# Where the 64-place and the 32-place expert stand in the order of a routed feed-forward stage

## The chip, the cores and the metric

One core of one Trainium2 chip runs the whole kernel as a single program. The metric is the device time of one execution in microseconds (us), from the device's own record; the median of several runs is compared. TensorE (PE in the rows, its weight loads PEld) does the matmuls, VectorE (DVE), ScalarE (ACT) and GpSimd (POOL) the rest, and SyncE's queue (SP) issues the loads of the weights.

## The reference

Two layers of a decoder on 256 tokens of width 1024, all in 32-bit floats. Each layer has a token mixer (four kinds of attention), a normalisation, a channel mixer, a normalisation and a small gated product with a per-layer embedding. The channel mixer of layer 0 is one dense SwiGLU. That of layer 1 is routed: every token goes to the best two of eight experts, and an expert is a SwiGLU of inner width 3584. Cut to what matters:

```python
def swiglu(x, w1, w3, w2):
    return (jax.nn.silu(x @ w1) * (x @ w3)) @ w2
...
        if i % 2 == 0:
            f = swiglu(h, ffn_w1[i // 2], ffn_w3[i // 2], ffn_w2[i // 2])
        else:
            f = moe_swiglu(h, moe_router[i // 2], moe_w1[i // 2], moe_w3[i // 2], moe_w2[i // 2])
        h = layer_norm(DEEPNORM_ALPHA * h + f, ln_ffn_g[i], ln_ffn_b[i])
        h = h + jax.nn.sigmoid(h @ ple_gate[i]) * (p[i] @ ple_proj[i])
```

All eight experts' weights (8 x 3 x 1024 x 3584 x 4 bytes, 352 MB) are read once from device memory.

## The kernel before, in words

The routed stage ranks the experts by how many tokens they got. The expert of rank r has `PLACES[r]` places for tokens: (128, 128, 96, 96, 96, 64, 32, 32). Ranks 0 and 1 are of class `Big`: their weights are split into a high and a low part (ACT line 103, DVE line 111) and each product is three matmuls (lines 142 to 144). The others are of class `Small`: plain 32-bit matmuls read the weights as they landed (line 1269 for `w1` and `w3`, line 1323 for `w2`). With fewer places than 128, one chunk of weights is worked on by several column groups of the array side by side (`q`: 4 groups of 32 places, or 2 of 64), so a chunk costs the less time the fewer places the expert has.

An expert is worked on in column steps of its inner width. A `Big` or 96-place expert has four steps (1024, 1024, 1024, 512 columns), a 64- or 32-place expert two (2048, 1536). `STEPS` lists pairs (rank, step) in the order of the work. One turn of the loop over `STEPS` does, in this order: `up` with `w1` of its own step (in its middle, `turn_last` transposes the previous step's result, lines 1194 and 1294); SiLU on ACT; `down` with `w2` of the *previous* step; `up` with `w3` of its own step and the scaling by the gates; then `make_for(s)`, which prepares an expert that comes later (`gather`: the tokens' rows are picked by matmuls with a 0/1 matrix, lines 1134 and 1135, transposed, line 1140, and the gates are gathered, line 1108); then `finish_last`, which puts an expert's result back to its tokens (`put_back`, lines 1117 and 1340, added to the residual by `add_back` on DVE, line 1353), if the previous step was that expert's last. The recording layer interleaves such pieces into the matmuls around them.

The tokens `x` of an expert lie in a tile `xg` (two halves for two experts each) or, for 32 places, in a tile `xe`. The `xg` tiles of the 96- and 64-place experts use the memory of the `Big` experts' tiles, so none of them can be made before the last matmul of (1,3) with `w3` has read those. After the last step `closing()` loads what the end of layer 1 needs, `put_back` of the last expert follows, a branch (line 1441) leads round a fallback for a fuller routing, and the second normalisation and the embedding product end the kernel.

The weights come in 348 chunks of 1 MB, or 768 KB for the second step's `w1` and `w3` of 64- and 32-place experts, all issued by SP's queue in the order of use (line 87; two pieces of 512 KB each from line 1314 where a group's rows don't lie together). `load_raw` takes twelve buffers (`raw` 4, `side` 3, `post` 3, `early` 2) in a fixed rotation: a chunk's load waits until the chunk twelve places ahead of it has been used. A chunk of either size takes a whole buffer.

Of the kernel before, what the change touches and what calls it, by code (L numbers as in the profile page):

```python
# [22 lines left out]
D_FF, N_EXP = 3584, 8  # L23
NFC = D_FF // 512
PLACES = (128, 128, 96, 96, 96, 64, 32, 32)
STEPS = ((0, 0), (7, 0), (0, 1), (0, 2), (0, 3), (1, 0), (7, 1), (1, 1), (1, 2), (1, 3), (6, 0), (2, 0),
         (2, 1), (2, 2), (2, 3), (6, 1), (3, 0), (3, 1), (3, 2), (5, 0), (3, 3), (4, 0), (4, 1), (4, 2),
         (4, 3), (5, 1))
PLE = 256
ALPHA = (2 * DEPTH) ** 0.25  # L30
EPS = 1e-5
# [22 lines left out]
def body(ctx, tc, nc, I, out):  # L54
# [932 lines left out]
    def swiglu_moe(hT, logits, closing):  # L987
        hh, hl = hT
        with tc.tile_pool(name="moe", bufs=1, reuse_waits="tile") as mp:
# [131 lines left out]
            def gather(r, n, off, x):  # L1121


                oh = places(r, n, off)
                if off == 0 and r == 0:
                    with tc.issue_after(done["oh"].ins):
                        gates()
                        ranks()
                xs = mp.tile([128, D], FT, name="xs", tag="xs", bufs=1)
                for f in range(2):  # L1130
                    fs = slice(f * 512, (f + 1) * 512)
                    p = work()
                    for t in range(NT):
                        nc.tensor.matmul(p[:n], oh[:, t], hsh[:, t, fs], start=t == 0, stop=False)
                        nc.tensor.matmul(p[:n], oh[:, t], hsl[:, t, fs], start=False, stop=t == NT - 1)
                    nc.scalar.activation(xs[:n, fs], p[:n], AF.Copy)
                for k0 in range(0, KD, 4):
                    p = work()[:, :4 * n].rearrange("p (a b) -> p a b", a=4)
                    for j in range(4):
                        nc.tensor.transpose(p[:, j], xs[:n, (k0 + j) * 128:(k0 + j + 1) * 128], ident[:n, :n])  # L1140
                    if n == 128:
                        ins = split_sb(x[0][:, k0:k0 + 4], x[1][:, k0:k0 + 4], p)
                    else:
                        nc.scalar.activation(x[:, k0:k0 + 4], p, AF.Copy)
                if off == 0 and r == 0:
                    table("silu_and_others", ins)
                gs = mp.tile([128, 3], FT, name="gs", tag="gs", bufs=3)
                if n == 128:
                    gates_of(r, oh, gs[:, :1])
                    return gs, back_of(oh)  # L1150
                w = 64 if n == 64 else 32
                for j in range(n // w):
                    gates_of(r, places(r, w, off + j * w, 128 // w), gs[:, j:j + 1])
                return gs, None
# [205 lines left out]
            def experts_in(base, order):  # L1360
                sizes = [128] * N_EXP if base else PLACES
                seq = STEPS if base == 0 else [(r, c) for r in range(N_EXP) for c in range(len(Big.cols))]
                first = {}
                for s, (r, c) in enumerate(seq):
                    first.setdefault(r, s)
                made = {}

                xg = {}

                def half(kind, i, j):  # L1370
                    if kind not in xg:
                        xg[kind] = [pers.tile([128, KD, 256], kind, name="xg", tag=tag) for tag in ("hTh", "hTl")]
                    return xg[kind][i][:, :, j * 128:(j + 1) * 128]

                def make(r):
                    n = sizes[r]
                    if n == 128:
                        x = [half(FR, i, r % 2) for i in range(2)]
                    elif n > 32:
                        x = half(FT, r in (3, 4), r in (4, 5))  # L1380
                    else:
                        x = mp.tile([128, KD, 32], FT, name="xe", tag="xe", bufs=1)
                    if n < 128:
                        x = x[:, :, :n]
                    got = gather(r, n, PLACES[r] if base else 0, x)
                    made[r] = Big(r, x, got) if n == 128 else Small(r, x, got, n)

                def make_for(s):
                    for r, f in first.items():
                        if f and max(f - 2, 0) == s and r not in made:  # L1390
                            make(r)

                make(seq[0][0])
                if base == 0:
                    order.enter_context(tc.issue_after(done["oh"].ins))
                    order.enter_context(tc.issue_after(done["hs"].ins))
                if base == 0:
                    for t in range(NT):
                        nc.vector.tensor_scalar(h[:, t], h[:, t], ALPHA, None, op0=OP.mult)
                before_ = g = gT = None  # L1400

                def turn_last():
                    nonlocal gT
                    if g is not None:
                        gT = before_[0].turn(g, before_[1])

                def finish_last():
                    ex, c = before_
                    if c == len(ex.cols) - 1:
                        ex.put_back()  # L1410

                for s, (r, c) in enumerate(seq):
                    now = made[r]
                    ps = now.up("moe_w1", c, turn_last)
                    sl = mp.tile([128, 1024], FT, name="sl", tag="sl")
                    for f, p in enumerate(ps):
                        nc.scalar.activation(sl[:, f * 512:f * 512 + p.shape[1]], p, AF.Silu)
                    if before_ is not None:
                        before_[0].down(gT, before_[1])
                    elif s == 0:  # L1420
                        make_for(s)
                    now.scale(sl, now.up("moe_w3", c))
                    if before_ is not None:
                        make_for(s)
                        finish_last()
                    g, before_ = sl, (now, c)
                    if s == 0 and base == 0:
                        turn_last()
                        now.down(gT, c)
                        g = before_ = None  # L1430
                turn_last()
                before_[0].down(gT, before_[1])
                rest = closing() if base == 0 else None
                finish_last()
                if rest is not None:
                    rest()
# [12 lines left out]
    for i in range(DEPTH):  # L1449
        hT, got = mixer(i, hT, None if i else second)  # L1450
        with tc.tile_pool(name=f"post{i}", bufs=1, reuse_waits="tile") as pool:
# [7 lines left out]
            else:  # L1459
# [7 lines left out]
                def closing():  # L1467

                    for n in ("early", "post", "side"):
                        del rings[n]  # L1470
                    n = PLE // 128 * S
                    words = held()
                    kept["p"] = [words[:, j * n:(j + 1) * n].rearrange("p (k s) -> p k s", s=S).bitcast(FR)
                                 for j in range(2)]
                    ple_turn(i, pool.tile([128, NT, PLE], FT, name="pt", tag="sg", bufs=1), *kept["p"])
                    kept["proj"] = ple_weights(i, held)
                    raw = load_raw(gate_weights(i, 0)[:, :4], [128, 4, 512])
                    kept["gb"] = load_gb("ffn", i, halves(held()))
                    kept["gate"] = []

                    def split(u):
                        wh, wl = split_unit(raw[:, u:u + 2], held, nc.gpsimd)
                        kept["gate"] += [(wh[:, j], wl[:, j]) for j in range(2)]

                    split(0)
                    return lambda: split(2)
# [47 lines left out]
```

## Time and profile before

| what | value |
|---|---|
| median of 3 runs | 1522.1 us (1520.16 to 1522.77) |
| the profiled execution's own time | 1520.21 us |
| its span in the profile | 1518.4 us |
| PE busy | 1429.0 us, 94% of the span |
| DVE, ACT busy | 681.5 us (45%), 563.0 us (37%) |
| loads by SP's queue | 455.5 MB, packets busy 77.5% of 16 engines' span |
| mean granted clock of TensorE | 0.97 |

The profiled execution took 1.8 us more than its span, and 1.9 us less than the median of the runs. Shares are averages over a span with several stages; the routed stage runs from about 600 to 1472 us.

### The profile page before, as it was taken

The numbers are of one execution on the slowest core, as the hardware profiler recorded it, in microseconds if no ns is written. First come the engines' busy times: TensorE is split into PE (matmuls) and PEld (weight loads), VectorE is DVE, ScalarE is ACT, GpSimd is POOL, SyncE is SP. The second block draws the span as 40 slices with busy tenths as digits, with TensorE's granted clock in tenths as the row PEclk, the third lists the DMA queues.
The fourth block names the chain that finished last, engine by engine and source line by source line (L and its number), as shares of the span: only waits on it lengthen the run. The fifth ranks groups of instructions, "written<-read, shape, count | busy, mean of one in ns | idle before, by whom it ended". The sixth has DMA issues, their size and how long they took to land. (4 is left out here: it accounts for less than half of the span.)

```text
span 1518.4 us, 29609 instructions
## 1 busy us (share of the span) xinstructions
PE 1429.0 (94%) x12545; PEld 993.4 (65%) x12545; DVE 681.5 (45%) x1167; ACT 563.0 (37%) x877; POOL 9.3 (1%) x16
## 2 busy tenths in 40 slices
PE   7999899999999997979999799899899999999988
PEld 6677788888786775647876575365745544566536
DVE  7666654554776768527885584100111000010035
ACT  5465544444554566426754573000000000000024
POOL 0000000000000000000000000000000000000000
PEclk9999999999999998998999899999989999999999
DMA  8543655464256543999999998999999999999963
GB/s 288 212 153 132 222 195 193 166 204 156 99 169 219 189 153 115 374 416 412 407 377 406 411 410 354 415 411 409 388 411 410 412 419 411 408 412 398 365 237 112
DMA packets 125963, 457.46 MB, mean 301 GB/s; under 512 B 11072, under 2 KB 22144, under 8 KB 104832
## 3 DMA queue, kind: packets, MB, share of 16 engines
q1 hardware_dynamic: 125824, 455.50, 77.5%
q8 instruction: 101, 1.65, 0.5%
q14 instruction: 38, 0.31, 0.1%
HBM read 454.42 MB, written 1.05 MB: 300 GB/s over the span
## 5 line engine op out<-in xcount | busy, mean ns | idle before, releaser
L111 DVE TENSOR_TENSOR wlo<-raw,whi 128x1024 fp32r<-128x1024 f32 (+1 forms) x152 | 181.0, 1211 | 82.2 <-ACT whi L103 77.4
L103 ACT ACTIVATE whi<-raw 128x1024 fp32r<-128x1024 f32 (+1 forms) x152 | 155.9, 1051 | 109.3 <-PE acc L143 53.0
L1278 DVE SCALAR_TENSOR_TENSOR sl<-sl,gs,wk 128x256 f32<-128x256 f32 (+3 forms) x44 | 19.3, 486 | 353.5 <-PE wk L1269 353.4
L1295 ACT ACTIVATE ge<-wk 128x512 f32<-128x512 f32 (+2 forms) x29 | 13.5, 503 | 321.3 <-PE wk L1294 321.3
L1269 PE MATMUL wk<-raw,xg 128*32 128x256 f32 (+3 forms) x1800 | 104.9, 362 | 4.3 <-issue 3.6
L142 PE MATMUL wk<-whi,xg 128*128 128x512 f32 x224 | 92.2, 412 | 9.8 <-ACT whi L103 7.5
L111 DVE TENSOR_TENSOR wlo<-post,whi 128x1024 fp32r<-128x1024 f32 x70 | 84.2, 1220 | 32.8 <-ACT whi L103 31.1
L142 PE MATMUL acc<-whi,gh 128*128 128x512 f32 x224 | 88.5, 396 | 5.0 <-ACT whi L103 4.0
L103 ACT ACTIVATE whi<-post 128x1024 fp32r<-128x1024 f32 x70 | 72.6, 1057 | 54.1 <-PE wk L143 32.0
L142 PE MATMUL wk<-whi,hTh 128*128 128x512 f32 x224 | 88.6, 396 | 3.1 <-ACT whi L103 3.1
L143 PE MATMUL wk<-whi,xg 128*128 128x512 f32 x224 | 91.2, 407 | 0.0
L111 DVE TENSOR_TENSOR wlo<-side,whi 128x1024 fp32r<-128x1024 f32 x72 | 86.4, 1219 | 10.5 <-ACT whi L103 5.5
L144 PE MATMUL wk<-wlo,hTh 128*128 128x512 f32 x224 | 88.0, 394 | 0.1
L143 PE MATMUL acc<-whi,gl 128*128 128x512 f32 x224 | 87.9, 393 | 0.0
L143 PE MATMUL wk<-whi,hTl 128*128 128x512 f32 x224 | 87.6, 391 | 0.0
L1269 PEld LDWEIGHTS wk<-raw,xg 128*32 128x32 f32 (+1 forms) x1800 | 58.3, 112 | 42.1 <-issue 14.7
L144 PE MATMUL wk<-wlo,xg 128*128 128x512 f32 x224 | 84.2, 410 | 0.9 <-DVE wlo L111 0.8
L144 PE MATMUL acc<-wlo,gh 128*128 128x512 f32 x224 | 84.5, 394 | 0.3
L103 ACT ACTIVATE whi<-side 128x1024 fp32r<-128x1024 f32 x72 | 74.5, 1056 | 19.9 <-PE acc L143 12.0
L142 PE MATMUL acc<-whi,hTh 128*128 128x512 f32 (+1 forms) x192 | 77.1, 402 | 1.4 <-ACT whi L103 1.4
L144 PE MATMUL acc<-wlo,hTh 128*128 128x512 f32 (+1 forms) x192 | 76.5, 399 | 1.4 <-DVE wlo L111 1.4
L1269 PE MATMUL wk<-side,xg 128*32 128x256 f32 (+2 forms) x1216 | 73.6, 365 | 4.0 <-issue 4.0
(404 smaller groups left out, 2504.8 us busy)
## 6 DMA issues: line engine op xcount, KB each, us to landing
raw<-in_moe_w_dram SPq DMA_DIRECT2D x96, 1024.0 KB, 17.9
side<-in_moe_w_dram SPq DMA_DIRECT2D x73, 1024.0 KB, 17.8
post<-in_moe_w_dram SPq DMA_DIRECT2D x72, 1024.0 KB, 16.9
early<-in_moe_w_dram SPq DMA_DIRECT2D x49, 1024.0 KB, 17.6
raw<-in_ffn_w_dram SPq DMA_DIRECT2D x19, 1024.0 KB, 5.1
raw<-in_w_in_dram SPq DMA_DIRECT2D x15, 1024.0 KB, 7.8
post<-in_ffn_w_dram SPq DMA_DIRECT2D x14, 1024.0 KB, 5.0
raw<-in_moe_w_dram SPq DMA_DIRECT2D x17, 768.0 KB, 10.9
```

The costliest lines, as they stand in the source:

```text
L103: nc.scalar.activation(hi, v, AF.Copy)
L111: engine.tensor_sub(lo, v, hi.bitcast(FT))
L142: nc.tensor.matmul(ps, xh, wh, start=first, stop=False)
L143: nc.tensor.matmul(ps, xl, wh, start=False, stop=False)
L144: return nc.tensor.matmul(ps, xh, wl, start=False, stop=last)
L1269: nc.tensor.matmul(ps[b][self.rows(u), at:at + wd], self.x[:, k, self.block(j)], raw[:, k % m, u * w + o:u * w + o + wd], start=k == 0 and ...
L1278: nc.vector.scalar_tensor_tensor(sl[:, fs], sl[:, fs], self.gs[:, j:j + 1], ps[b][:, at:at + wd], op0=OP.mult, op1=OP.mult)
L1295: nc.scalar.activation(gT[:, j0:j0 + m], p, AF.Copy)
```

## The change

Ranks 5 (64 places) and 6 (32 places) swap their places in `STEPS`, so that the 64-place steps stand behind (1,3) and behind (2,3), and the 32-place steps stand ahead of (4,0) and at the end. (3,3) no longer has another expert's step ahead of it. In `make_for` the expert of rank 5 is made one step ahead of its first step, not two, because its tile needs the memory that (1,3) still reads. No size, no buffer and no arithmetic on any expert changes.

```diff
-STEPS = ((0, 0), (7, 0), (0, 1), (0, 2), (0, 3), (1, 0), (7, 1), (1, 1), (1, 2), (1, 3), (6, 0), (2, 0),
-         (2, 1), (2, 2), (2, 3), (6, 1), (3, 0), (3, 1), (3, 2), (5, 0), (3, 3), (4, 0), (4, 1), (4, 2),
-         (4, 3), (5, 1))
+STEPS = ((0, 0), (7, 0), (0, 1), (0, 2), (0, 3), (1, 0), (7, 1), (1, 1), (1, 2), (1, 3), (5, 0), (2, 0),
+         (2, 1), (2, 2), (2, 3), (5, 1), (3, 0), (3, 1), (3, 2), (3, 3), (6, 0), (4, 0), (4, 1), (4, 2),
+         (4, 3), (6, 1))
...
-                        if f and max(f - 2, 0) == s and r not in made:
+                        if f and (f - 1 if r == 5 and not base else max(f - 2, 0)) == s and r not in made:
```

First place: PE at the seam between (1,3) and the step behind it. `xg_4858` and `xg_4859` are the `Big` tiles, `oh` the 0/1 matrix, `xs` the gathered rows. Before, the seam holds the end of making expert 2 and then the 32-place step's first matmuls:

```order
L144 MATMUL wk_7478<-wlo_7514,xg_4858 128x512
L1135 MATMUL wk_7530<-hsl_4816,oh_7526 96x512
L1134 MATMUL wk_7536<-hsh_4815,oh_7526 96x512
L1135 MATMUL wk_7536<-hsl_4816,oh_7526 96x512
L1134 MATMUL wk_7536<-hsh_4815,oh_7526 96x512
L1135 MATMUL wk_7536<-hsl_4816,oh_7526 96x512
L1140 MATMUL wk_7542<-ident_69,xs_7529 128x96 x4
L1140 MATMUL wk_7548<-ident_69,xs_7529 128x96 x4
L1108 MATMUL wk_7558<-gate_r_4855,oh_7555 128x1 x2
L1108 MATMUL wk_7565<-gate_r_4855,oh_7562 128x1 x2
L1108 MATMUL wk_7572<-gate_r_4855,oh_7569 128x1
L1269 MATMUL wk_7576<-raw_7577,xe_7290 32x512
```

At the same place of the changed kernel, the end of making expert 5 comes first and then the making of expert 2; behind these rows come one more of line 1140, the gates of line 1108 and then the 64-place step's first matmuls (line 1269, `raw,xg`, 64x512):

```order
L1140 MATMUL wk_7505<-ident_69,xs_7492 128x64 x4
L1140 MATMUL wk_7511<-ident_69,xs_7492 128x64 x4
L1108 MATMUL wk_7521<-gate_r_4855,oh_7518 128x1 x2
L1134 MATMUL wk_7529<-hsh_4815,oh_7525 96x512
L1135 MATMUL wk_7529<-hsl_4816,oh_7525 96x512
L1134 MATMUL wk_7529<-hsh_4815,oh_7525 96x512
L1135 MATMUL wk_7529<-hsl_4816,oh_7525 96x512
L1134 MATMUL wk_7535<-hsh_4815,oh_7525 96x512
L1135 MATMUL wk_7535<-hsl_4816,oh_7525 96x512
L1134 MATMUL wk_7535<-hsh_4815,oh_7525 96x512
L1135 MATMUL wk_7535<-hsl_4816,oh_7525 96x512
L1140 MATMUL wk_7541<-ident_69,xs_7528 128x96 x4
```

Expert 5 is now made here, one step ahead of its use, where expert 6 had been made one step earlier, and expert 2 is made whole between the two.

Second place: PE at the end of the routed stage, `down` of the last step and `put_back` of its expert. Before, with 64 places:

```order
L1294 MATMUL wk_12542<-ident_69,sl_12335 128x128 x2
L1323 MATMUL acc_10767<-post_12546,ge_12535 64x512 x4
L1323 MATMUL acc_10767<-raw_12552,ge_12535 64x512 x4
L1323 MATMUL acc_10767<-raw_12558,ge_12535 64x512 x4
L1323 MATMUL acc_10767<-side_12564,ge_12535 64x512 x4
L1323 MATMUL acc_10767<-post_12570,ge_12535 64x512 x4
L1323 MATMUL acc_10767<-early_12576,ge_12535 64x512 x4
```

The changed kernel has 32 places there:

```order
L1294 MATMUL wk_12502<-ident_69,sl_12304 128x128 x3
L1323 MATMUL acc_11069<-post_12507,ge_12501 32x256 x8
L1323 MATMUL acc_11069<-raw_12517,ge_12501 32x256 x8
L1323 MATMUL acc_11069<-raw_12527,ge_12501 32x256 x8
L1323 MATMUL acc_11069<-side_12538,ge_12501 32x256 x8
L1323 MATMUL acc_11069<-post_12548,ge_12501 32x256 x8
L1323 MATMUL acc_11069<-early_12558,ge_12501 32x256 x8
```

The six last chunks are the same in number and buffers, and each now has eight matmuls of 256 columns in four column groups instead of four of 512 columns in two. `put_back` behind them has 16 matmuls of 256 columns and eight `add_back` of 128x256 where it had eight of 512 columns and four of 128x512.

## Rows read from the trace of the kernel before

**Rows 1.** The page, 40 slices of the span: mean DMA rate

```profile
GB/s 288 212 153 132 222 195 193 166 204 156 99 169 219 189 153 115 374 416 412 407 377 406 411 410 354 415 411 409 388 411 410 412 419 411 408 412 398 365 237 112
```

**Rows 2.** Windows of 20 us: busy us by engine, granted clock, DMA share, GB/s

```profile
920.00:940.00 20.00, 18.67 (x109) 10.45 (x111) 4.31 (x14) 2.65 (x5) 0.00 (x0) 0.91 0.76 301
...
980.00:1000.00 20.00, 17.15 (x260) 9.22 (x256) 1.03 (x3) 0.00 (x0) 0.00 (x0) 0.83 1.02 408
1000.00:1020.00 20.00, 20.00 (x358) 11.93 (x354) 0.23 (x1) 1.74 (x4) 0.00 (x0) 1.00 1.02 415
...
1400.00:1420.00 20.00, 18.93 (x461) 13.78 (x455) 0.00 (x0) 1.36 (x3) 0.00 (x0) 1.00 1.00 386
1420.00:1440.00 20.00, 17.50 (x179) 8.36 (x174) 0.86 (x3) 1.36 (x3) 0.00 (x0) 0.91 0.92 346
```

**Rows 3.** PE's timeline, neighbouring chunks of one size: start us, us

```profile
957.25 1.04 PE L1269 MATMUL wk<-raw,xe 128*32 128x512 f32 x8
958.11 1.04 PE L1269 MATMUL wk<-side,xe 128*32 128x512 f32 x8
...
1428.10 1.46 PE L1269 MATMUL wk<-post,xg 128*64 128x512 f32 x8
1429.39 1.46 PE L1269 MATMUL wk<-early,xg 128*64 128x512 f32 x8
...
1468.94 1.89 PE L1323 MATMUL acc<-post,ge 128*64 128x512 f32 x8
1470.66 1.89 PE L1323 MATMUL acc<-early,ge 128*64 128x512 f32 x8
```

**Rows 4.** SP's timeline, DMA issues (us to landing), PE's timeline: first chunk of (6,0)

```profile
886.61 0.34 SPq L87 DMA_DIRECT2D raw<-in_moe_w_dram  x1
...
raw<-in_moe_w_dram SPq DMA_DIRECT2D x1, 1024.0 KB, 18.3
...
920.81 13.58 SPq L87 DMA_DIRECT2D raw<-in_moe_w_dram  x2
...
930.88 1.04 PE L1269 MATMUL wk<-raw,xe 128*32 128x512 f32 x2
```

**Rows 5.** PE's timeline with its waits: `w2` of (6,0), first and last wait

```profile
974.49 1.07 PE L1323 MATMUL acc<-side,ge 128*32 128x256 f32 x16 [1.23 <-DMA side<-in_moe_w_dram]
...
987.14 4.34 PE L1269 MATMUL wk<-post,xg 128*32 128x256 f32 x48 [1.59 <-DMA post<-in_moe_w_dram]
```

**Rows 6.** The same three views: first chunks of (6,1) and of (5,1)

```profile
1060.19 8.96 SPq L87 DMA_DIRECT2D post<-in_moe_w_dram  x1
...
post<-in_moe_w_dram SPq DMA_DIRECT2D x1, 768.0 KB, 19.3
...
1097.21 0.83 PE L1269 MATMUL wk<-post,xe 128*32 128x384 f32 x2
...
1390.01 5.75 SPq L87 DMA_DIRECT2D raw<-in_moe_w_dram  x1
...
raw<-in_moe_w_dram SPq DMA_DIRECT2D x1, 768.0 KB, 16.1
...
1423.78 2.82 PE L1269 MATMUL wk<-raw,xg 128*64 128x512 f32 x8 [2.50 <-issue]
```

**Rows 7.** The same views at the end: last weights, then PE and DVE

```profile
1446.15 0.33 SPq L87 DMA_DIRECT2D early<-in_moe_w_dram  x1
...
early<-in_moe_w_dram SPq DMA_DIRECT2D x1, 1024.0 KB, 11.8
...
1472.48 0.66 PE L280 MATMUL wk<-ident,pt 128*128 128x128 f32 x4
...
1474.93 0.49 PE L1340 MATMUL wk<-yl,ohT 64*128 64x512 f32 x2
...
1481.14 0.68 DVE L1353 SCALAR_TENSOR_TENSOR h<-h,wk 128x512 f32<-128x512 f32 x1
...
1482.03 0.77 PE L142 MATMUL acc<-early 128*128 128x512 f32 x1 [6.62 <-DVEq L1441]
```

## The prediction

> **What bounds the kernel now.** I began with the slices of the page [rows 1]. From about slice 17 on, roughly 600 us into the span, the weights arrive at some 410 GB/s almost without a break until the last slices: the routed stage is bound by its stream of weights. Then I read windows of 20 us, to see where the stream falls short of that [rows 2]. An undisturbed window moves 415 GB/s at a DMA share of 1.02; the stretch 920 to 940 only 301, and 1400 to 1440 only 386 and 346. Such dips have one kind of cause here, and the reader sees it at the first of them [rows 4]: SP's queue stands for 13.58 us from 920.81 on, because the buffer that its load wants is still in use by PE. PE was far behind. The first chunk of (6,0) was issued at 886.61 and landed 18.3 us later, at 904.9, but its first matmul starts at 930.88. I call that distance PE's *lag* behind the stream: 26.0 us. With twelve buffers a lag of that size leaves nothing to load into.
>
> So the stage has two ledgers. The stream ends when all chunks have been moved at 410 GB/s, plus every us in which no buffer was free. And PE ends some lag after the stream. Last I read the end [rows 7]: the last weights were issued at 1446.15 and landed 11.8 us later, at 1458.0, while PE finished with them at 1472.5. The end of the stage is therefore set by PE, 14.5 us behind the stream.
>
> **The price of a chunk.** At 410 GB/s a chunk of 1 MB takes the stream 2.56 us and one of 768 KB 1.92 us. On PE, by the distance of neighbouring starts [rows 3], 1 MB takes 0.86 us with 32 places and 1.72 with 64, and 768 KB takes 1.29 us with 64. So every such chunk lets PE catch up, a 32-place chunk by 1.70 us, a 64-place one by 0.84. The arithmetic of all experts is the same before and after; the change only moves where PE catches up, and 24 chunks of a first step are worth 40.8 us of it with 32 places, 20.2 with 64.
>
> **At the end: the gain.** The last step (6,1) takes 0.86 us a chunk against 2.56 of the stream, so PE will be waiting for each of the last chunks and be done one chunk's work after the last landing: 0.9 us behind instead of 14.5. If the stream ended when it does now, that would be 13.6 us gained. Bounds of that lag: 0.9, and 4 if the transposes of the step's result come late.
>
> **Behind (1,3): the lag that stays.** Before, PE went through the 24 chunks of (6,0) (and `w1` of (2,0) and `w2` of (1,3) among them) and its lag fell from 26.0 to nothing: from 974.49 to 987.14 it waited six times for a chunk, 6.1 us in all [rows 5]. So part of that catching up was wasted. The ledger closes as follows: 26.0, plus what PE did besides in this stretch, less 40.8 caught up, less the stream's own loss (20 us at 301 instead of 410 GB/s is 5.3) must give -6.1; the rest is 14.0 us. With (5,0) there instead: 26.0 + 14.0 - 20.2 - 5.3 = 14.5 us of lag at `w3` of (2,0), where it is now nothing. Making expert 5 in front of the step instead of expert 6 a step earlier adds no new kind of work: its matmuls take the place of similar ones that already stood ahead of 930.88. But buffers come free at 1.72 instead of 0.86 us a chunk while the queue stands. For that I take s1 = 2 us of further loss (bounds 0, since 1.72 is still quicker than the stream, and 3). The lag left is then about 12.5.
>
> **Ahead of (5,1): the first price.** In the trace of before, PE's lag grew from nothing at 987 to 17.7 at the start of (6,1) [rows 6]: that chunk was issued at 1060.19, landed at 1079.5, and was used at 1097.21. Expert 2 and the making of expert 3 stand there unchanged. 12.5 + 17.7 = 30.2 us is more than the buffers allow. At 26.0 the queue stands [rows 4], so at least 4.2 us are lost. And (5,1) brings chunks of 768 KB, which fill a whole buffer with less stream: where they were the next to load, a lag of 17.7 was already enough to take the stream to 346 GB/s (the first chunk of (5,1) was issued at 1390.01, landed 16.1 later, used at 1423.78 [rows 6, 2]). Down to that level it would be 12.5 us lost. I take s2 = 9, since a window of mixed sizes lies between the two levels and nearer to the small chunks: 26.0 x 0.75 is 19.5, from which 30.2 stands off by 10.7.
>
> **Ahead of (6,0): the second price.** Expert 3 now runs its four steps in one piece, without the 64-place step that stood between (3,2) and (3,3), and expert 4 is made directly in front of (6,0), as expert 2 was in front of (6,0) before. No row gives the lag that it comes with. The nearest is that very dip, 5.3 us; I take s3 = 5 (bounds 0, if the lag is still under 20, and 7, with two more us for the making).
>
> **What goes away.** The losses of 1400 to 1440 belong to (5,1) with a PE that was 17.7 behind: 20 x (410 - 386)/410 + 20 x (410 - 346)/410 = 1.2 + 3.1 = 4.3 us. Behind (6,0) PE is close to the stream, so most of it should go: 3 us (bounds 0 and 4.3).
>
> **The sum.** The stream ends at 1458.0 + 2 + 9 + 5 - 3 = 1471.0, and PE at 1471.9 instead of 1472.5: -0.6 us. In the tail, `put_back` of the 32-place expert has eight `add_back` of 256 columns where four of 512 took 0.68 each [rows 7]; at most the double, 2.7 us more, at least nothing. The closing loads now come right behind weights that PE waits for, and no longer 14 us ahead of the branch at 1482.03. I take 1.3 us for both together. That makes +0.7 us: 1520.9 against the profiled 1520.2. The profiled execution lies 1.9 us under the median of the runs, so against the median the forecast is 1522.8 us: no change that can be told. What a measurement of this kernel can tell from no change is about 0.2%, 3 us.
>
> **A clock rule that speaks against the change.** Where PE waited for single chunks, its clock fell: the window 980 to 1000 has a granted clock of 0.83, so for a third of it PE ran at 1.2 instead of 2.4 GHz [rows 2, 5]. The Trainium skill, "TensorE: Matmul & The Clock Gate", section "HAM oscillation — how this bites in real kernels", describes this pattern: a loop whose matmuls are done before the next tile of weights has come drops to the low clock in the wait and starts each next tile slow. The trace agrees. Here the last 32-place step is such a loop. At the low clock a chunk takes 1.72 us, still under 2.56, so only the last chunk (+0.9) and the matmuls of `put_back` would show, which stand between 1472.48 and 1475.4 with a pause among them [rows 7]: 2 us more at the most. That is some +3 us on the sum, 1525.8.
>
> **Rivals.** *The buffers absorb it (0.25).* If the lag ahead of (5,1) is only carried and worked off, what is left of s1, s2, s3 is the necessary 4.2, and the loss at the end goes: 1458.0 + 4.2 - 3 = 1459.2, PE at 1460.1, 12.4 earlier, less 1.3 in the tail: 1511.0; with s1 as well 1513.0, in the middle 1512.0. For it: while the lag grew from nothing to 17.7, the stream moved its 415 GB/s [rows 2]. Against: at 26.0 it stood. *The middle costs more than the end gives (0.20).* One mechanism, at one place: the 768 KB chunks of (5,1). If the queue stands until the lag is down to 17.7, s2 is 12.5 and the stream then meets (6,0) with the full s3 of 7: 2 + 12.5 + 7 - 3 = 18.5, PE ends at 1477.4, +4.9 and 1.3, 1528.3; with s1 at 3 and nothing gone away at the end, 1532. It decides where the losses together pass 12.3 us (13.6 less the tail's 1.3). *The low clock at the end (0.10)*: 1525.8, as above. *The exchange as summed: 0.45*, 1519.8 to 1525.8.
>
> **How the numbers follow.** Faster by over 0.2%: the first rival and a little of the exchange, 0.28. Slower: the second rival, most of the third, 0.29. Within: 0.43. The range goes from the first rival's 1512 to the second's 1530; beyond them I leave a part of each, together under 0.2. The exchange's own range is 1519.8 to 1525.8.
>
> **What would show it.** In the profile of the changed kernel: the last weights land at about 1471 and PE is done with them within 2 us, with a wait for DMA ahead of each of the last chunks; no wait for DMA in `w2` of (5,0), where there were six; dips of the GB/s ahead of (5,1), some 1080 to 1120, and ahead of (6,0), some 1240 to 1280; none at 1400 to 1440. The forecast is wrong if the dip ahead of (5,1) is under 4 us or over 13, or if the end still shows PE more than 4 us behind.

## The result: slower by 0.6%

| | before | changed |
|---|---|---|
| median | 1520.75 us (1516.69 to 1522.77, 6 runs) | 1528.55 us (1525.41 to 1532.05, 6 runs) |
| ratio, 95% interval | | 1.0057 (1.0036 to 1.0078) |
| profiled execution | 1520.21 us, span 1518.4 | 1528.78 us, span 1527.0 |

The kernel became 7.8 us slower by the medians, 8.6 us by the two profiled spans. The forecast was 1522.8 us with a range of 1512 to 1530: the time lies in the range, near its upper end, but outside the exchange's own 1519.8 to 1525.8. It stands at the second rival (the middle costs more than the end gives, 1528.3 us).

The windows of 20 us of the changed kernel, with the columns of [rows 2], show where the stream of weights stood:

```profile
920.00:940.00 20.00, 18.25 (x76) 10.11 (x76) 3.75 (x17) 3.41 (x7) 0.00 (x0) 0.74 0.51 195
940.00:960.00 20.00, 18.29 (x74) 9.01 (x70) 6.09 (x7) 6.66 (x9) 0.00 (x0) 0.91 1.00 404
...
1080.00:1100.00 20.00, 18.97 (x464) 14.03 (x466) 0.00 (x0) 1.36 (x3) 0.00 (x0) 1.00 0.95 360
1100.00:1120.00 20.00, 18.67 (x118) 10.01 (x109) 2.99 (x14) 2.54 (x5) 0.00 (x0) 0.83 0.58 195
...
1240.00:1260.00 20.00, 19.68 (x398) 14.10 (x394) 2.26 (x8) 2.97 (x7) 0.00 (x0) 1.00 0.97 370
1260.00:1280.00 20.00, 18.20 (x358) 14.89 (x350) 2.44 (x11) 2.06 (x4) 0.00 (x0) 1.00 0.89 342
1280.00:1300.00 20.00, 18.68 (x190) 7.33 (x189) 2.92 (x11) 3.11 (x7) 0.00 (x0) 0.92 0.84 329
...
1400.00:1420.00 20.00, 20.00 (x458) 14.24 (x454) 1.26 (x3) 1.36 (x3) 0.00 (x0) 1.00 1.03 403
1420.00:1440.00 20.00, 17.79 (x390) 12.01 (x383) 0.86 (x3) 0.49 (x1) 0.00 (x0) 1.00 1.02 410
...
1460.00:1480.00 20.00, 12.93 (x136) 4.69 (x135) 2.60 (x9) 1.70 (x5) 0.00 (x0) 0.83 1.02 406
```

The last column is the one to read. Measured against 410 GB/s, the first pair loses 10.5 + 0.3 us where the kernel before lost 5.3 [rows 2]; the second pair 2.4 + 10.5 us, where the same windows of before moved 382 and 398 GB/s, 2.0 us; the third group 2.0 + 3.3 + 4.0 us, where the kernel before, at 418, 412 and 405 GB/s, lost nothing. And 1400 to 1440, 4.3 us short before, is now 0.3 short. Together 5.5 + 10.9 + 9.3 - 4.0 = 21.7 us more are lost than before.

The rows of the changed kernel that answer to [rows 4] and [rows 7], from SP's timeline, the DMA issues (us to landing) and PE's timeline:

```profile
883.07 0.35 SPq L87 DMA_DIRECT2D raw<-in_moe_w_dram  x1
...
raw<-in_moe_w_dram SPq DMA_DIRECT2D x1, 1024.0 KB, 18.6
...
919.66 17.04 SPq L87 DMA_DIRECT2D raw<-in_moe_w_dram  x2
...
931.27 1.97 PE L1269 MATMUL wk<-raw,xg 128*64 128x512 f32 x2
...
1069.68 2.02 SPq L87 DMA_DIRECT2D post<-in_moe_w_dram  x1
...
post<-in_moe_w_dram SPq DMA_DIRECT2D x1, 768.0 KB, 12.4
...
1106.62 1.97 PE L1269 MATMUL wk<-post,xg 128*64 128x512 f32 x2
...
1238.03 0.34 SPq L87 DMA_DIRECT2D post<-in_moe_w_dram  x1
...
post<-in_moe_w_dram SPq DMA_DIRECT2D x1, 1024.0 KB, 10.7
...
1278.71 0.62 PE L1269 MATMUL wk<-post,xe 128*32 128x512 f32 x1
...
1461.55 0.33 SPq L1314 DMA_DIRECT2D early<-in_moe_w_dram  x1
...
early<-in_moe_w_dram SPq DMA_DIRECT2D x1, 512.0 KB, 15.6
...
1472.16 1.94 PE L1323 MATMUL acc<-side,ge 128*32 128x256 f32 x16 [2.41 <-DMA side<-in_moe_w_dram]
1474.65 1.93 PE L1323 MATMUL acc<-post,ge 128*32 128x256 f32 x16 [0.56 <-DMA post<-in_moe_w_dram]
...
1478.10 0.66 PE L280 MATMUL wk<-ident,pt 128*128 128x128 f32 x4
...
1489.59 0.77 PE L142 MATMUL acc<-early 128*128 128x512 f32 x1 [8.99 <-DVEq L1441]
```

The first chunk of (5,0) landed at 901.7 and was used at 931.27, a lag of 29.6 us where it had been 26.0, and the queue stood for most of 17.04 us (that row, like the one of 13.58 us in [rows 4], holds two issues and the stand between them). The first chunk of (5,1) landed at 1082.1 and was used at 1106.62, a lag of 24.5; that of (6,0) landed at 1248.7 and was used at 1278.71, a lag of 30.0. At the end the last piece of the weights landed at 1461.55 + 15.6 = 1477.15, and PE was done with it at 1478.1: the lag of 14.5 us has become 1 us, and PE waits for single chunks. But the landing is 19.2 us later than the 1458.0 of before, and measured from the first chunk of the first exchanged step (901.7 against 904.9) 22.4 us later, which the 21.7 us of the windows account for. These 3.2 us of a head start are no part of the change: in `w2` of (7,1), ahead of everything that was changed, PE's wait for a `post` chunk ended at 835.33 in this execution and at 838.54 in that of before. PE's end moved by 5.6 us, from 1472.5 to 1478.1. The other 3.0 us of the span lie behind that: PE's first matmul behind the branch follows its last one of `w2` by 11.5 us where it was 9.5, and the rest of the tail takes another us.

The lag at (5,0) is longer because PE's way to it is. From those two waits on, PE needed 92.3 us to the first chunk of (6,0) before and 95.9 us to that of (5,0) in the changed kernel. The making of expert 2 had run among the last matmuls of (1,3); now expert 5 is made there, and expert 2 behind it, alone. The last matmul of (1,3), first before, then in the changed kernel, and two windows of the changed kernel with the columns of [rows 2]:

```profile
925.86 0.40 PE L144 MATMUL wk<-wlo,xg 128*128 128x512 f32 x1
...
920.79 0.39 PE L144 MATMUL wk<-wlo,xg 128*128 128x512 f32 x1
...
925.00:930.00 5.00, 4.51 (x20) 3.63 (x18) 1.03 (x5) 2.17 (x4) 0.00 (x0) 0.50 0.47 195
930.00:935.00 5.00, 4.46 (x12) 1.98 (x13) 1.07 (x6) 0.00 (x0) 0.00 (x0) 0.50 0.00 0
```

From there to the first chunk it is 10.5 us where it was 5.0. From 925 to 935 the granted clock is at its lower level, 0.50, after PE had gone over from the matmuls of (1,3) to the small ones of making the two experts. Three other kernels with the same order there (`e2_5665`, `e6_after_early6` and `e9_after_late` below) have 0.83 instead of 0.74 in the window 920 to 940, a third less time at the low clock, and lose 9.6 to 9.9 us in it against 10.5; so that third is worth under one us.

### The profile page after: what moved, and what is told of

The parts are those of the page before. It is cut to its first block, busy times and chain, and to the rows that moved or that the text cites. A ratio compares the mean times of both kernels' runs of the same rounds, so it can differ in the third digit from the quotient of the medians.

```text
span 1527.0 us, 29608 instructions
## 1 busy us (share of the span) xinstructions
PE 1434.4 (94%) x12545; PEld 992.7 (65%) x12545; DVE 680.4 (45%) x1167; ACT 562.9 (37%) x877; POOL 8.1 (1%) x16
## 3 DMA queue, kind: packets, MB, share of 16 engines
HBM read 454.42 MB, written 1.05 MB: 298 GB/s over the span
## 5 line engine op out<-in xcount | busy, mean ns | idle before, releaser
L1269 PE MATMUL wk<-raw,xg 128*32 128x256 f32 (+2 forms) x1672 | 104.8, 371 | 0.7 <-DMA raw<-in_moe_w_dram 0.7
L1269 PEld LDWEIGHTS wk<-raw,xg 128*32 128x32 f32 (+1 forms) x1672 | 56.2, 113 | 38.4 <-issue 11.5
L1269 PE MATMUL wk<-post,xg 128*32 128x256 f32 (+3 forms) x1216 | 76.7, 366 | 0.0
```

The source lines that it names most:

```text
L1269: nc.tensor.matmul(ps[b][self.rows(u), at:at + wd], self.x[:, k, self.block(j)], raw[:, k % m, u * w + o:u * w + o + wd], start=k == 0 and ...
```

## The experiments

Two theories were set against each other. **Theory A** is that of the prediction: the stage ends with its stream, every us in which the queue stands is lost, and PE's lag at the end can be won back. **Theory B** reads the same trace from PE's side: PE's work is the same in any order, so only PE's waits for weights can be gained or lost, and a standing queue costs nothing while PE has work. Slots are named by the ranks in the four places of `STEPS` where a rank of 5 or 6 stands: 6, 6, 5, 5 before; 5, 5, 6, 6 in the changed kernel. A ratio is taken against the kernel before on the same chip; where the medians of two kernels are compared directly, they can come from different chips, on which the kernel before had medians of 1519.52 to 1520.75 us.

**Other orders.** `e1_6556` takes the slots 6, 5, 5, 6, with the third between (3,2) and (3,3) as before, and `make_for` as before:

```diff
-         (2, 1), (2, 2), (2, 3), (6, 1), (3, 0), (3, 1), (3, 2), (5, 0), (3, 3), (4, 0), (4, 1), (4, 2),
-         (4, 3), (5, 1))
+         (2, 1), (2, 2), (2, 3), (5, 0), (3, 0), (3, 1), (3, 2), (5, 1), (3, 3), (4, 0), (4, 1), (4, 2),
+         (4, 3), (6, 1))
```

> Order of the four slots 6, 5, 5, 6: the 32-place step again behind (1,3), both 64-place steps in the middle, the 32-place step at the end as in the changed kernel. Theory A (that of the prediction: the stage ends with its stream, which loses every us that the load queue stands, and a 32-place end wins back PE's lag of 14.5 us): the first seam loses only its 5.3 us again, the two later ones about 6 each, the end is won: about 6 us under the kernel before, some 1515 us. Theory B (PE is the bound all along: the stage takes PE's work plus PE's own waits for weights; a standing queue costs nothing while PE has work, and the lag at the end is no reserve): the six waits behind (1,3), 6 us, are there as in the kernel before, and those at the end as in the changed kernel, with its later tail: 5 to 9 us over the kernel before, 1526 to 1530 us.

Measured: 1514.78 us against 1520.29, ratio 0.9974 (0.9955 to 0.9993). `e2_5665` takes 5, 6, 6, 5 (here against the changed kernel, whose `make_for` it keeps):

```diff
-         (2, 1), (2, 2), (2, 3), (5, 1), (3, 0), (3, 1), (3, 2), (3, 3), (6, 0), (4, 0), (4, 1), (4, 2),
-         (4, 3), (6, 1))
+         (2, 1), (2, 2), (2, 3), (6, 0), (3, 0), (3, 1), (3, 2), (6, 1), (3, 3), (4, 0), (4, 1), (4, 2),
+         (4, 3), (5, 1))
```

> Order of the four slots 5, 6, 6, 5: the 64-place step behind (1,3) as in the changed kernel, the 32-place steps in the middle, the 64-place step at the end as in the kernel before. Theory A (stream): the first seam loses 5.5 us more than before, the second about 4, and the end keeps PE's lag of 14.5 us: some 8 us over the kernel before, 1529 us. Theory B (PE): no wait for weights behind (1,3), since the lag stays at some 13 us, none at the end, and few in the middle, where the lag is high when the 32-place steps come: up to 6 us under the kernel before, 1515 to 1518 us.

Measured: 1526.83 us, ratio 1.0045 (1.0032 to 1.0058). Theory A named both times to within 2.2 us, and theory B had the wrong sign both times. The ends are as A has them: PE is done with `w2` 0.7 us behind the last landing in the order 6, 5, 5, 6 (1464.2 against 1463.5) and 14.3 us in the other (1478.3 against 1464.0). The places of A's losses are not: in the order 6, 5, 5, 6 the two later seams lose 3.0 us (1100 to 1120, 349 GB/s) and 1.9 us (1220 to 1260, 393 and 388) instead of 6 each, and 7.5 us are lost from 1380 to 1440 (375, 342 and 360), of which the expectation says nothing. So that this time came out right is in part luck. What failed in B was not its account but its guess where PE would wait. In the order 5, 6, 6, 5 PE's waits in expert 3 and its neighbours, from 1130 to 1330, are (the lines of these two kernels stand two lower than in the listing):

```profile
PE acc L1321 <- DMA raw<-in_moe_w_dram: 3.9, 4, 1.4
PE wk L1267 <- DMA raw<-in_moe_w_dram: 3.5, 3, 1.7
PE acc L1321 <- DMA side<-in_moe_w_dram: 2.9, 2, 1.9
PE acc L1321 <- DMA post<-in_moe_w_dram: 2.0, 2, 1.4
PE wk L1267 <- DMA post<-in_moe_w_dram: 1.0, 1, 1.0
```

These columns are us in total, times, longest us: 13.3 us of waits for weights, where the kernel before has 6.1 us behind (1,3) [rows 5] and none from 1130 to 1330. The 32-place steps stand there at a lag that is already low, so what they let PE catch up is thrown away, after the queue had stood for it at the first seam. That is the link between the two accounts, as far as this trace shows it: a stall of the stream at a high lag comes back as a wait of PE at the next place where the lag runs out.

**A part of expert 4 left out.** Both kernels leave out 7 of the 28 row groups of `w2` of rank 4; all loads stay:

```diff
                     self.left -= 1
+                    if self.r == 4 and self.n == 32 and self.left % 4 == 1:
+                        return
```

> The kernel before, in which expert 4 leaves out one of four of its w2 products (7 of 28 row groups, 9.1 us of PE at 1.3 us each); loads unchanged. Theory B (PE): 9 us less, about 1512 us, since nothing after expert 4 waits for weights. Theory A (stream): the same 9 us less here, as PE stays behind the stream at the end. A third theory, that the routed stage is bound by its stream alone and PE's lag is only an appearance: no change.

> The changed kernel with the same part of expert 4 left out (7 of 28 row groups of w2, 9.1 us of PE). Theories A and B: PE is already level with the stream from expert 4 on and waits for the last chunks, so the 9 us turn into longer waits: 0 to 2 us less than the changed kernel, 1526 to 1529 us. If it falls by 9 us, the end of the changed kernel is not set by the stream.

Measured: 1508.67 us for the kernel before (ratio 0.9903, 0.9878 to 0.9927), 11.6 us less by the medians and 9.0 by the profiled spans; 1530.12 us for the changed one (ratio to the kernel before 1.0070, 1.0055 to 1.0085), no less than its 1528.55 (by the spans 1.6 us less). So PE's work set the end of the kernel before, and in the changed kernel the work of expert 4 no longer sets it. A bound by the stream alone, in both, is excluded.

**Where expert 2 is made.** `e5_after_m2`, `e8_6556_m2` and `e10_before_m2` move one thing in three orders, the making of expert 2 to one step ahead of its use, behind the step that follows (1,3):

```diff
-                        if f and (f - 1 if r == 5 and not base else max(f - 2, 0)) == s and r not in made:
+                        if f and (f - 1 if r in (2, 5) and not base else max(f - 2, 0)) == s and r not in made:
```

(with `r == 2` in the other two orders).

> The changed kernel, with expert 2 made one step later (behind the matmuls of (5,0) with w3, no longer between (1,3) and (5,0)). Theory A1 (the stream stands behind (1,3) because PE has the making of two experts to do before it can free the first buffer): the loss of the window 920 to 960 falls from some 11 us to 5 or 6, and the kernel is 3 to 5 us faster than the changed one, some 1524 us. Theory A2 (it stands because 64-place chunks come free at 1.72 instead of 0.86 us): the loss stays at 9 to 11, no change, 1528 us.

> The order 6, 5, 5, 6 with expert 2 made one step later, behind (6,0) with w3. Theory A1 (making expert 2 in front of the first buffer that comes free makes the stream stand): the loss of 5.3 us in the window 920 to 940 goes down to 1 to 2, and PE waits less in w2 of (6,0): 3 to 4 us less than the order 6, 5, 5, 6, some 1511 us. If the loss is not the making, no change: 1515 us.

> The kernel before in its own order, with expert 2 made one step later only. Theory A1: the stream no longer stands behind (1,3) (window 920 to 940 at over 400 GB/s, where it had 301), PE waits 3 to 5 us less in w2 of (6,0): 3 to 5 us faster than before, some 1516 us. If the gain of this move hangs on the new order: no change.

Measured: 1522.82 us for the changed order (5.7 less than 1528.55), 1508.18 us for 6, 5, 5, 6 (6.6 less than 1514.78), 1513.75 us for the order of before (ratio 0.9966, 0.9952 to 0.9979). The windows behind (1,3), first of the changed order with this edit, then of the order before with it:

```profile
920.00:940.00 20.00, 19.23 (x94) 8.25 (x92) 3.47 (x8) 2.87 (x6) 0.00 (x0) 1.00 1.01 415
940.00:960.00 20.00, 17.93 (x80) 9.31 (x80) 7.06 (x13) 7.10 (x11) 0.00 (x0) 1.00 1.02 415
960.00:980.00 20.00, 19.61 (x200) 9.66 (x204) 5.09 (x16) 1.08 (x2) 0.00 (x0) 1.00 0.94 362
980.00:1000.00 20.00, 20.00 (x182) 8.02 (x176) 0.00 (x0) 0.87 (x2) 0.00 (x0) 1.00 0.98 377
```

```profile
920.00:940.00 20.00, 18.28 (x116) 9.86 (x116) 6.07 (x6) 5.33 (x7) 0.00 (x0) 1.00 1.01 420
940.00:960.00 20.00, 19.11 (x170) 9.96 (x166) 6.92 (x22) 2.78 (x6) 0.00 (x0) 0.91 1.02 414
```

The stand behind (1,3) is gone in both, and A1 is confirmed against A2: 64-place chunks alone do not make the queue stand there. What held the first buffer was the making of expert 2 between (1,3) and the step that frees it. With it the fall of the clock is gone too (1.00 in the changed order from 920 to 1000), so the runs don't separate the two. In the changed order 3.9 us of the loss come back from 960 to 1000, where expert 2 is now made at a lag that is still high.

**Where the 32-place step stands in expert 3.** `e6_after_early6` puts (6,0) between (3,2) and (3,3):

```diff
-         (2, 1), (2, 2), (2, 3), (5, 1), (3, 0), (3, 1), (3, 2), (3, 3), (6, 0), (4, 0), (4, 1), (4, 2),
+         (2, 1), (2, 2), (2, 3), (5, 1), (3, 0), (3, 1), (3, 2), (6, 0), (3, 3), (4, 0), (4, 1), (4, 2),
```

> The changed kernel, with (6,0) one place earlier, between (3,2) and (3,3), where the kernel before had (5,0); expert 4 is then made one step behind it. Theory A1 (the third loss, some 9 us between 1240 and 1300, comes from making expert 4 directly ahead of (6,0) at a high lag): the loss falls to 2 to 5 us and the kernel is 3 to 6 us faster than the changed one, 1523 to 1526 us. If it is only expert 3 without relief that fills the buffers, the loss stays and so does the time.

Measured: 1521.87 us, 6.7 less than the changed kernel and not told from the kernel before (ratio 1.0011, 0.9998 to 1.0023). Its windows there:

```profile
1240.00:1260.00 20.00, 20.00 (x294) 9.84 (x290) 1.27 (x3) 1.47 (x3) 0.00 (x0) 1.00 1.00 407
1260.00:1280.00 20.00, 19.02 (x224) 9.75 (x216) 2.13 (x11) 2.06 (x4) 0.00 (x0) 0.91 1.02 410
1280.00:1300.00 20.00, 14.45 (x316) 10.00 (x312) 0.75 (x1) 1.09 (x2) 0.00 (x0) 0.98 1.02 419
```

The third loss of 9.3 us has gone but for 1.1 us, which now stand at 1220 to 1240 (388 GB/s); that is more than was expected. The step and the making of expert 4 both changed places here, so the run says that their place makes the loss, not which of the two makes more of it.

**The tail.** In the order 6, 5, 5, 6 PE ends the stage 8.3 us earlier than before, but its first matmul behind the branch comes 13.0 us behind its last of `w2`, where it was 9.5. DVE's timeline there, ahead of the branch and behind it:

```profile
1471.24 0.41 DVE L1351 SCALAR_TENSOR_TENSOR h<-h,wk 128x256 f32<-128x256 f32 x1
...
1471.70 1.35 DVE L1347 TENSOR_TENSOR sums<-quarters 128x4 f32<-128x4 f32 x1
1477.11 0.21 DVE L384 TENSOR_SCALAR lnnm<-sums 128x1 f32<-128x1 f32 x1 [4.07 <-DVEq L1439]
```

`e7_6556_dve` does the embedding gate's splits on DVE, so that POOL has no work there:

```diff
-                        wh, wl = split_unit(raw[:, u:u + 2], held, nc.gpsimd)
+                        wh, wl = split_unit(raw[:, u:u + 2], held)
```

> The order 6, 5, 5, 6 with the two splits of the embedding gate's weights on DVE instead of POOL. In the profile of the order 6, 5, 5, 6 the stage's last matmul of w2 ends 8 us earlier than before but the span only 3.5 us; the branch comes 13 us behind it instead of 9.5. Theory T1 (DVE's last small add, 1.35 us where it takes 0.16 elsewhere, and the branch behind it wait for POOL's splits): the tail gets 2 to 3 us shorter, some 1512 us. Theory T2 (the tail waits for the closing loads): no change or 1 us slower, since DVE has 2.4 us more to do: 1515 us.

Measured: 1515.12 us, no change. By the total alone T1 would not have to fall, since DVE now does two splits of 1.2 us more; the trace decides it. Without POOL the small add takes 0.16 us again, but DVE still goes on only 2.4 us behind it, so T1 falls:

```profile
1473.86 0.16 DVE L1349 TENSOR_TENSOR sums<-quarters 128x4 f32<-128x4 f32 x1
1476.44 0.21 DVE L386 TENSOR_SCALAR lnnm<-sums 128x1 f32<-128x1 f32 x1 [2.43 <-DVEq L1441]
```

That left the add itself. A 32-place `put_back` sums a row in four quarters and adds them up at its end (line 1349); a 64-place one does not. `e9_after_late` and `e11_6556_m2_late` let all `add_back` write the quarters, and add them up once behind the branch:

```diff
-                    if w < 512:
-                        nc.vector.tensor_add(sums, quarters[:, :, :2], quarters[:, :, 2:])
...
             with tc.If(flag > 0):
                 experts(1)
+                nc.vector.memset(quarters[:, :, 2:], 0.0)
+            nc.vector.tensor_add(sums, quarters[:, :, :2], quarters[:, :, 2:])
```

> The changed kernel, with the sum of the row-sum quarters (DVE's last instruction ahead of the branch, line 1349) moved behind the branch. Theory T3 (this add waits for DVE's own add_backs, holds DVE's queue and so puts the branch, 2.4 to 4 us, behind the end of put_back, where a 64-place expert at the end has no such add): the tail from the last w2 matmul to the first matmul behind the branch falls from 11.5 to some 9 us, and the kernel is 2 to 3 us faster than the changed one, 1526 us. If the tail waits for the closing loads or for POOL instead: no change, 1528.5 us.

> The order 6, 5, 5, 6, expert 2 made one step later, and the sum of the quarters behind the branch. Theory T3: 2 to 3 us less than without the last edit, about 1506 us; if the tail waits for something else, 1508 us.

Measured: 1526.13 us and 1505.63 us, 2.4 and 2.6 us less than without the edit; the intervals of the ratios overlap (1.0049 against 1.0057, 0.9918 against 0.9934), so the totals alone don't settle it. The tail does, in one trace of each: from PE's last `w2` matmul to its first behind the branch, the changed kernel with this edit takes 8.6 us where it took 11.5 (and the other order 9.0 where it took 13.3):

```profile
1476.47 1.12 PE L280 MATMUL wk<-ident,pt 128*128 128x128 f32 x4
...
1485.04 0.76 PE L142 MATMUL acc<-early 128*128 128x512 f32 x1 [5.30 <-ACTq L1439]
```

**Experts 3 and 4 later too.** `e12_6556_m234_late` widens the rule of the last kernel to `r in (2, 3, 4)`:

> As the kernel of that order with the late sum, and experts 3 and 4 made one step later too. Theory A1: the loss ahead of (5,0), some 2 to 3 us in 1060 to 1140, shrinks, since expert 3 is no longer made in front of the first buffer that comes free; but PE's lag is under the buffers' limit in most of this order, so little comes of it: 0 to 3 us less, 1503 to 1506 us.

Measured: 1504.80 us, ratio 0.9907 (0.9886 to 0.9929), against 1505.63: no difference that can be told. The loss ahead of (5,0) did go: 1080 to 1120 moves 416 and 414 GB/s, where the kernel without it moved 376 and 408. But as much came back behind it: 375 at 1140 to 1160, where that kernel moved 407. It is the fastest median of the study, 14.7 us under the kernel before.

## Why the prediction held in its range and missed in its middle

- **What bounds the kernel; the two ledgers.** Right: the end of the changed kernel hangs on its stream, and the order 6, 5, 5, 6 and its reverse took the times that the stream's ledger gave, though in the first the losses stood at other places.
- **At the end: the gain of 13.6 us.** Right: the lag went from 14.5 to 1 us, 13.5 us.
- **The lag that stays behind (1,3).** Right: in `w2` of (5,0) PE waits for no chunk, where before it had waited six times in that stretch, and at `w3` of (2,0), whose first chunk was issued at 978.75, landed 9.9 us later and was used at 1001.89, the lag is 13.2 us where 12.5 was forecast. But s1 was too small, 5.5 us and not 2. The step that failed is that making expert 5 there "adds no new kind of work", because its matmuls take the place of similar ones: PE's way to the first chunk became 3.6 us longer, and the lag there went from 26.0 to 29.6. The runs with expert 2 made later show that the slower freeing costs nothing by itself. How the 5.5 us divide while expert 2 is made there, between the longer way, the lower clock in it and the slower freeing, was not tried.
- **The first price, ahead of (5,1).** The place was right, and the size was 10.9 and not 9 us. The queue stood at a lag of 24.5 us, under the 26.0 at which it stood with chunks of 1 MB, as the mechanism of the smaller chunks asks; but how much of the loss is their size was not tried by itself. In the order 6, 5, 5, 6 the making of expert 3 was what was left of that loss.
- **The second price, ahead of (6,0).** The step that was most mis-sized: 9.3 us and not 5, beyond the upper bound of 7 that it was given. The price was copied from the dip behind (1,3), and the lag that (6,0) comes with was never worked out; the lower bound even had it under 20. It was 30.0 us, above the 26.0 at which that dip lost its 5.3. That the place makes the loss is shown by the run with (6,0) one place earlier.
- **What goes away.** 4.0 and not 3 us.
- **The tail.** 3.0 and not 1.3 us. Neither of the two reasons given, the number of `add_back` and the closing loads, was the main one; that was the small add in front of the branch, without which the way to the branch took 8.6 us, less than the 9.5 of before.

In sum the middle cost 21.7 and not 13 us of stream, against an end that gave what was forecast. The second rival's own path, 18.5 us of stream and 1528.3 us, was the closest: it had the larger losses ahead of (5,1) and (6,0), though not the one behind (1,3). The line that was to tell it from the exchange, losses of 12.3 us, does not: the exchange's own 13 us lie past it. Nor did the forecast's signs of being wrong watch the place that missed most: they name the dip ahead of (5,1), which was 12.9 us in all and so just under its 13, and the end, but not the dip ahead of (6,0) or the sum.

That the time lies in the range is in part luck. The change forecast for the profiled execution was +0.7 us, and the spans show +8.6, beyond the exchange and beyond the second rival's +6.2. What brings the times together is the 1.9 us that were added because the profiled execution lay that much under the first median: beside the later medians it lies 0.5 us under (1520.21 and 1520.75), and that of the changed kernel 0.2 us over (1528.78 and 1528.55). Without the 1.9 us the second rival stands at 1526.4 us and the upper end of the range at 1528.1, under the measured time.

The rival of the low clock at the end was seen, with 0.83 in the window 1460 to 1480 and `w2` chunks of 1.94 instead of 1.07 us, but it lies inside the waits, and only the last chunk shows. The Trainium skill's "TensorE: Matmul & The Clock Gate", section "HAM oscillation — how this bites in real kernels", was cited for that pattern; the trace agrees with the pattern and gives it a price of some 0.8 us here: the last chunk took 1.81 us, where it took 1.05 in the order 6, 5, 5, 6.

## What to carry to other kernels

Write down how far the engine is behind its loads at each seam, and beside it the lag at which no buffer is free. Here a light step was worth only the lag that it found, and nothing once the lag was gone, while more work for PE at full buffers cost the stream at once. Work that only a later step needs should not stand between full buffers and the instruction that frees the first of them: moving one such piece was worth 6 us in each of three orders, as much as the whole reordering. And when the last work ahead of a branch changes its kind, look at what the engine that is seen to release the branch has last in its queue.

## What the runs showed of the hardware

A small add of 128x4 on DVE, ahead of the branch, took 0.82 to 1.35 us beside two splits on POOL, and 0.16 us without them. The Trainium skill, "SBUF — State Buffer", section "Who interferes with whom", says that a DVE instruction with two inputs in SBUF contends with one of GpSimd that reads SBUF; these rows agree. With that add as the last instruction ahead of the branch, DVE went on 2.4 to 4.1 us later. With `add_back` as the last it went on 0.15 us later in the trace of before (from 1481.83 to 1481.98) and in that of `e9_after_late`, but 1.4 us later in that of `e11_6556_m2_late` and 1.7 us in that of `e12_6556_m234_late`. In every trace with the add PE's way from its last `w2` matmul to the branch is longer, 11.3 to 13.3 us against 8.6 to 9.6 in those without it; why, and what DVE waits for in the last two, the runs do not show.
